# A gated delta rule inside a two-block network: readers of solved blocks queued behind the weights, the last solve level applied to the values, decay rows broadcast by DMA

## The chip, the cores and the metric

The kernel runs on one core of a Trainium2 chip. The metric is the device time of one execution in microseconds; the program has no second core to wait for. The engines are named as in the profile: PE is TensorE, DVE is VectorE, ACT is ScalarE, POOL is GpSimd, SP is the engine whose queue issues most DMAs. PEld is the weight load of PE.

## The reference, cut to what matters

Two transformer-like blocks over 256 tokens of width 2048. The change touches only the gated delta rule of the first block: 8 heads of dimension 128, chunks of 64 in the reference (the kernel takes chunks of 128, two per head).

```python
def chunk_gated_delta_rule(q, k, v, g, beta):
    ...
    gc = jnp.cumsum(g, axis=-1)
    gamma = jnp.exp(jnp.where(causal, gc[..., :, None] - gc[..., None, :], -jnp.inf))
    kb = k * beta[..., None]
    a_mat = jnp.where(strict, jnp.einsum('bhncd,bhnsd->bhncs', kb, k) * gamma, 0.0)
    t_mat = lax.linalg.triangular_solve(eye + a_mat, eye, left_side=True, lower=True, unit_diagonal=True)
    u = jnp.einsum('bhncs,bhnsv->bhncv', t_mat, v * beta[..., None])
    w = jnp.einsum('bhncs,bhnsk->bhnck', t_mat, kb * jnp.exp(gc)[..., None])
    qk = jnp.einsum('bhncd,bhnsd->bhncs', q, k) * gamma
    ...
    def step(state, xs):
        v_new = u_n - jnp.einsum('bhck,bhkv->bhcv', w_n, state)
        o = jnp.einsum('bhck,bhkv->bhcv', qg_n, state) + jnp.einsum('bhcs,bhsv->bhcv', qk_n, v_new)
        state = state * gl_n[..., None, None] + jnp.einsum('bhck,bhcv->bhkv', kd_n, v_new)
```

q, k and v come from a matmul, a causal convolution of width 4 and SiLU; q and k are l2-normalised per token. The result is rms-normed, multiplied by SiLU(z) and projected. Around it stand an attention branch, a feed-forward block, and a second block with sparse attention and retention, all untouched.

## The kernel before

All large weights stream from DRAM in granules of 128 x 1024 fp32. `load_w` takes each granule through three steps: an SP DMA into `w` (4 buffers), an ACT copy to the rounded half `wh` (3 buffers), a DVE subtraction to the rest `wl` (4 buffers). One output chunk of 128 x 256 is two granules and 48 matmuls (`wh` with both halves of the activations, `wl` with one).

**The order on PE is written out by hand.** Everything that is not a weight matmul (the delta rule, attention) is a generator; `tick` runs one step of one due generator after each group of three weight matmuls. A generator says with `yield x` when it is due next, in planner microseconds. The planner's clock advances with each matmul by columns / 2400 us, times 4 for plain fp32. So a chunk is 5.12 planner microseconds. `finish(t)` runs generators, jumping the clock to their due times with no weight matmul between, until `t` is done. The other engines' queues are ordered by a scheduler that has its own estimate of each duration and puts an instruction where it believes it to be ready; each engine then works its queue strictly in order. `behind()` adds an edge: an instruction of the block comes after the last traced granule's instruction on the same engine.

**The delta rule.** For each head `gdn_scores` squares k and q (ACT), sums the squares over the head dimension by four one-column matmuls (`tok_sums`, into `cs`), makes the decay rows `pr` by two matmuls with the gate column broadcast as weights, adds the mask, exponentiates them into `gam`, and multiplies k·k and k·q (`k0`, `k1`) by them into `S`. Four heads form a group. `gdn_solve` moves the 32 x 32 diagonal blocks of the group's S through DRAM into `X` on 32 partitions (POOL DMAs), eliminates them in 30 steps of two POOL instructions (L805, L806), and moves them back into S (L808, L810). Its planner distances are 8 for the way in, 1.3 a step, 8 for the way back. Then `gdn` runs per head: `level(0)` masks the solved blocks out of S (DVE, L829), DE = I - them (L834), PE transposes of DE, two merging levels (32 to 64 to 128), then the values: W0 = E0 V0, Y = V1 - S1 W0, W1 = E1 Y, the output `po`, its norm (with one POOL power, `f`), and transposes back. Heads 0 and 1 of a group run in lockstep, and heads 2 and 3 after them; each step is PE work and then an ACT or DVE instruction that reads its PSUM bank.

`mixers` runs group 0's scores, its values (and `a_block(1)`), group 1's scores, its values, `a_block(2)`, then the attention heads. `finish` of heads 0 and 1 of group 0 stands in front of the third head of group 1, because of S's three buffers.

Of the kernel before, what the change touches and what calls it, by code (L numbers as in the profile page):

```python
# [23 lines left out]
EPS = 1e-6  # L24
# [101 lines left out]
class Net:  # L126
# [386 lines left out]
    def mixers(self, bo, b1):  # L513
        nc, tmp, a = self.nc, self.tmp, self.a
# [74 lines left out]
        groups = []  # L589
        for p in range(2):  # L590
            hh = range(4 * p, 4 * p + 4)
            group = Group(hh)
            S = []
            for i, h in enumerate(hh):
                kq = b1.tile([P, 2, T], F32, tag="kq", name="kq", bufs=2)
                for j, dst in ((1, kq[:, 0]), (0, kq[:, 1])):
                    part(dst, j, h)
                if i >= 2:
                    self.finish(group.scores[i - 2])
                if i % 2 == 0:  # L600
                    if p and i:
                        for t in groups[0].heads[:2]:
                            self.finish(t)
                    S.append(b1.tile([P, 2, 6, P], F32, tag="gS", name="gS", bufs=3))
                group.scores.append(self.add(self.gdn_scores(h, kq, S[i // 2][:, i % 2], group)))
            group.solve = self.add(self.gdn_solve(S, group))
            for i, h in enumerate(hh):
                v = b1.tile([P, T], F32, tag="v", name="v", bufs=1)
                if p and i >= 1:
                    self.finish(groups[0].heads[i - 1])  # L610
                z = b1.tile([P, T], F32, tag="z", name="z", bufs=5)
                part(v, 2, h)
# [84 lines left out]
    def gdn_gates(self, ps, r):  # L697

        nc, b1 = self.nc, self.b1
        self.beta = b1.tile([P, H, 2], F32, name="beta")  # L700
        g = b1.tile([P, 2, H], F32, name="g")
        x = b1.tile([P, 2, H], F32, name="dl")
        e = b1.tile([P, 2, H], F32, name="de")
        for tt in range(2):
            nc.vector.tensor_scalar(self.beta[:, :, tt], ps[tt][:, 0:8], r[:, tt:tt + 1], None, op0=OP.mult)
            nc.vector.scalar_tensor_tensor(x[:, tt], ps[tt][:, 8:16], r[:, tt:tt + 1], self.row[:, 8:16],
                                           op0=OP.mult, op1=OP.add)
# [10 lines left out]
        self.g = g  # L718
        self.gcol = b1.tile([P, 3, H], F32, name="gcol")
        yield 10.0  # L720
        pc = self.aux([P, 3, H])
        lmid = self.c1("lcm")[:, P:2 * P]
        self.mm(pc[:, 0], lmid, g[:, 0])
# [8 lines left out]
    def gdn_scores(self, h, kq, S, pair):  # L732

        nc = self.nc
        sq = self.gtile(0, "sq", [P, 2, T])
        nc.scalar.activation(sq, kq, ACT.Square)
        yield 4.0 if h else 5.0

        pc = self.tok_sums([sq[:, 0], sq[:, 1]])
        cs = self.gtile(h, "cs", [P, 4])  # L740
        nc.vector.tensor_scalar(cs, pc, EPS, None, op0=OP.add)
        cp = self.b1.tile([P, 4], F32, tag="gcp", name="gcp", bufs=8)
        pair.cp[h] = cp
        self.pow(cp, cs, "mix")
        acol = self.gtile(h, "ac", [P, 2])
        nc.vector.reciprocal(acol, cs[:, 0:2])
        nc.vector.tensor_tensor(acol, acol, self.beta[:, h], op=OP.mult)

        pr = self.aux([P, 3, P])
        lcm = self.c1("lcm")  # L750
        g0 = self.g[:, 0, h:h + 1].to_broadcast([P, P])
        g1 = self.g[:, 1, h:h + 1].to_broadcast([P, P])
        self.mm(pr[:, 0], g0, lcm[:, P:2 * P])
        self.mm(pr[:, 1:3].rearrange("p a b -> p (a b)"), g1, lcm)
        gam = self.gtile(h, "gam", [P, 3, P])
        nc.vector.tensor_tensor(gam[:, 0::2], pr[:, 0::2], self.c1("gmask").unsqueeze(1).to_broadcast([P, 2, P]), op=OP.add)
        for i, j in ((0, 0), (1, 2), (2, 1)):
            nc.scalar.activation(gam[:, i], pr[:, 1] if i == 1 else gam[:, i], ACT.Exp, bias=self.gcol[:, j, h:h + 1])
        yield 2.5
        k0 = self.aux([P, 2, 2, P])  # L760
        kqf = kq.rearrange("p a t -> p (a t)")
        self.mm(k0.rearrange("p a b c -> p (a b c)"), kq[:, 0, 0:P], kqf)
        nc.vector.scalar_tensor_tensor(S.rearrange("p (x y) c -> p x y c", y=2)[:, 0::2], k0, acol[:, 0:1],
                                       gam[:, 0:2].unsqueeze(1).to_broadcast([P, 2, 2, P]), op0=OP.mult, op1=OP.mult)
        yield 0
        k1 = self.aux([P, 2, P])
        for i in range(2):
            self.mm(k1[:, 1 - i], kq[:, 0, P:T], kq[:, i, P:T])
        nc.vector.scalar_tensor_tensor(S[:, 2:4], k1, acol[:, 1:2],
                                       gam[:, 2:3].to_broadcast([P, 2, P]), op0=OP.mult, op1=OP.mult)  # L770

# [13 lines left out]
    def gdn_solve(self, S, group):  # L785


        nc, b1 = self.nc, self.b1
# [13 lines left out]
        for j in range(1, 31):  # L802
            t = tmp[:, 0:j * (31 - j)].rearrange("p (s c) -> p s c", s=j)
# [4 lines left out]
        nc.gpsimd.dma_start(Df, X)  # L808
        for d, y in diag:
            nc.gpsimd.dma_start(y, d)  # L810
        yield 8.0
        group.solved = True

    def gdn(self, h, S, group, before):
        nc, b1 = self.nc, self.b1
        z = group.z[h]
        tl = lambda tag, shape: self.gtile(h, tag, shape)
# [3 lines left out]
        cp, V = group.cp[h], group.V[h]  # L821

        B = S[:, 0::3]
        idb = self.c0("ident").unsqueeze(1).to_broadcast([P, 2, P])

        def level(l):
            m = self.lev[:, l * P:(l + 1) * P].unsqueeze(1).to_broadcast([P, 2, P])
            bm = tl("bm", [P, 2, P])
            nc.vector.tensor_tensor(bm, B, m, op=OP.mult)  # L829
            return bm  # L830

        bm = level(0)
        DE = tl("DE", [P, 2, 2, P])
        nc.vector.tensor_tensor(DE[:, 1], idb, bm, op=OP.subtract)  # L834
        yield 3.5
        pd = self.aux([P, 2, P])
        for tt in range(2):
            self.tr(pd[:, tt], DE[:, 1, tt])
        nc.scalar.copy(DE[:, 0], pd)
        for l in (1, 2):  # L840
            bm = level(l)
            yield 2.8
            pr = self.aux([P, 2, P])
            for tt in range(2):
                self.mm(pr[:, tt], bm[:, tt], DE[:, 0, tt])
            R = tl("R", [P, 2, P])
            nc.scalar.copy(R, pr)
            yield 2.4
            pu = self.aux([P, 2, 2, P])
            last = l == 2  # L850
            for tt in range(2):
                if not last:
                    self.mm(pu[:, 0, tt], DE[:, 1, tt], R[:, tt])
                self.mm(pu[:, 1, tt], R[:, tt], DE[:, 1, tt])
            if last:
                nc.vector.tensor_tensor(DE[:, 1], DE[:, 1], pu[:, 1], op=OP.subtract)
            else:
                nc.vector.tensor_tensor(DE, DE, pu, op=OP.subtract)
        E = DE[:, 1]
        W = tl("bm", [P, 2, P])  # L860
        yield 2.8
        pw = self.aux([P, P])
        self.mm(pw, E[:, 0], V[:, 0])
        nc.scalar.copy(W[:, 0], pw)
        yield 1.9
        px = self.aux([P, P])
        self.mm(px, S[:, 1], W[:, 0])
        Y = tl("Y", [P, P])
        nc.vector.tensor_tensor(Y, V[:, 1], px, op=OP.subtract)
        yield 1.9  # L870
        pw = self.aux([P, P])
        self.mm(pw, E[:, 1], Y)
        nc.scalar.copy(W[:, 1], pw)
        yield 1.9
        po = self.aux([P, 2, P])
        self.mm(po[:, 0], S[:, 4], W[:, 0])
        self.mm(po[:, 1], S[:, 5], W[:, 0], start=True, stop=False)
        self.mm(po[:, 1], S[:, 2], W[:, 1], start=False, stop=True)

        so = tl("so", [P, 2])  # L880
        dump = tl("Y", [P, P])
        for tt in range(2):
            nc.scalar.activation(dump, po[:, tt], ACT.Square, accum_out=so[:, tt:tt + 1])
        f = tl("f", [P, 2])
# [2 lines left out]
        nc.vector.tensor_scalar(so, so, SC * SC / P, EPS, op0=OP.mult, op1=OP.add)  # L887
        self.pow(f, so, "rsqrt")
        nc.vector.scalar_tensor_tensor(f, f, SC, cp[:, 2:4], op0=OP.mult, op1=OP.mult)
        on = tl("R", [P, 2, P])  # L890
        for tt in range(2):
            nc.scalar.mul(on[:, tt], po[:, tt], f[:, tt:tt + 1])
        yield 5.2
# [1 line left out]
        for tt in range(2):  # L895
            self.tr(pt[:, tt], on[:, tt])
        nc.vector.scalar_tensor_tensor(z, pt.rearrange("p a b -> p (a b)"), self.col("gnorm", 0), z,
                                       op0=OP.mult, op1=OP.mult)
# [573 lines left out]
```

## Time and profile before

| | us |
|---|---|
| median of 3 runs | 2533.32 (2533.11 to 2533.87) |
| the profiled execution | 2533.55 |
| its span | 2531.7 |
| PE busy | 2454.0 (97%) |
| DVE busy | 1905.9 (75%) |
| ACT busy | 1391.4 (55%) |
| POOL busy | 140.6 (6%) |

The span runs from the first to the last instruction of the profiled execution; its own time holds 1.85 us more around it. Busy time of PE is the time in which at least one matmul was under way. The delta rule lies in the first 500 us of the span.

### The profile page before, as it was taken

The numbers are of one execution on the slowest core, as the hardware profiler recorded it, in microseconds if no ns is written. First come the engines' busy times: TensorE is split into PE (matmuls) and PEld (weight loads), VectorE is DVE, ScalarE is ACT, GpSimd is POOL, SyncE is SP. The second block draws the span as 40 slices with busy tenths as digits, with TensorE's granted clock in tenths as the row PEclk, the third lists the DMA queues.
The fourth block names the chain that finished last, engine by engine and source line by source line (L and its number), as shares of the span: only waits on it lengthen the run. The fifth ranks groups of instructions, "written<-read, shape, count | busy, mean of one in ns | idle before, by whom it ended". The sixth has DMA issues, their size and how long they took to land.

```text
span 2531.7 us, 50856 instructions
## 1 busy us (share of the span) xinstructions
PE 2454.0 (97%) x20026; PEld 2438.4 (96%) x20026; DVE 1905.9 (75%) x3673; ACT 1391.4 (55%) x2208; POOL 140.6 (6%) x215
## 2 busy tenths in 40 slices
PE   8959779999999999999999999999999999999999
PEld 8959779999999999999999999999999999999999
DVE  7747567667788988888877678898888677666664
ACT  7626446544444556777754456654844556475443
POOL 0341610000000000000000000000000000000000
PEclk9979989999999999999999999999999999999999
DMA  6545474588898766766767767768677555455555
GB/s 219 192 148 168 137 229 143 183 266 300 295 299 297 225 223 209 239 221 210 243 215 211 242 216 218 216 211 266 211 245 236 179 183 174 152 169 171 176 184 159
DMA packets 190224, 536.66 MB, mean 212 GB/s; under 512 B 22176, under 2 KB 27680, under 8 KB 189984
## 3 DMA queue, kind: packets, MB, share of 16 engines
q1 hardware_dynamic: 188768, 532.36, 65.5%
q8 instruction: 157, 2.57, 0.4%
q0 software_dynamic: 1216, 1.05, 0.2%
q14 instruction: 83, 0.68, 0.1%
HBM read 530.70 MB, written 2.62 MB: 211 GB/s over the span
## 4 chain that ended last, share of the span: by engine, by line
PE 89%; DVE 3%; POOL 3%; DMA 2%; issue 1%; ACT 1%; SPq 0%; DVEq 0%; ACTq 0%; POOLq 0%
PE mm L186 84%; PE aux L186 4%; POOL gX L806 2%; POOL gXt L805 1%; DVE wl L223 1%; PE aux L190 1%; ACT wh L222 1%; DVE mw L1094 0%; DVE isc L1304 0%; DMA gX<-gD 0%; DMA w<-wA 0%; DMA gD<-gS 0%; DMA mc<-c 0%; DMA gD<-gX 0%; DMA mw<-wM 0%
## 5 line engine op out<-in xcount | busy, mean ns | idle before, releaser
L222 ACT CAST wh<-w 128x1024 fp32r<-128x1024 f32 (+5 forms) x867 | 854.0, 986 | 938.0 <-PE mm L186 771.4
L186 PE MATMUL mm<-u,wh 128*128 128x256 f32 (+1 forms) x7488 | 1361.9, 284 | 0.0
L223 DVE TENSOR_TENSOR wl<-w,wh 128x1024 fp32r<-128x1024 f32 (+5 forms) x867 | 993.6, 1147 | 400.6 <-ACT wh L222 396.1
L186 PEld LDWEIGHTS mm<-u,wh 128*128 128x128 f32 x7488 | 1152.8, 189 | 3.3 <-issue 2.4
L186 PE MATMUL mm<-u,wl 128*128 128x256 f32 (+1 forms) x3744 | 1053.9, 281 | 51.7 <-DVE wl L223 51.7
L186 PEld LDWEIGHTS mm<-u,wl 128*128 128x128 f32 x3744 | 706.9, 189 | 52.1 <-DVE wl L223 52.1
L186 PE MATMUL mm<-v,wh 128*128 128x256 f32 (+1 forms) x4096 | 743.4, 283 | 0.0
L186 PEld LDWEIGHTS mm<-v,wh 128*128 128x128 f32 x4096 | 629.3, 189 | 1.4 <-issue 1.0
L186 PE MATMUL mm<-v,wl 128*128 128x256 f32 (+1 forms) x2048 | 576.2, 281 | 1.6 <-DVE wl L223 1.4
L186 PEld LDWEIGHTS mm<-v,wl 128*128 128x128 f32 x2048 | 385.8, 188 | 2.6 <-DVE wl L223 2.6
L1094 DVE CUSTOM_DVE_ANT_0 mw<-mw,mc,mod 128x512 f32<-128x512 f32 x192 | 145.0, 759 | 2.9 <-ACT mc L1076 2.1
L1094 DVE CUSTOM_DVE_ANT_0 mw<-mw,mc,part 128x512 f32<-128x512 f32 x192 | 142.2, 747 | 2.7 <-ACT mc L1076 2.7
L186 PE MATMUL mm<-wh,u 128*128 128x412 f32 (+1 forms) x320 | 83.4, 339 | 0.0
L1052 ACT ACTIVATE leaf<-bit,row,dr 128x384 f32<-128x384 f32 x120 | 78.9, 699 | 0.0
L186 PE MATMUL mm<-wh,v 128*128 128x412 f32 (+1 forms) x256 | 71.8, 359 | 5.7 <-ACT wh L222 5.7
L694 DVE SCALAR_TENSOR_TENSOR u<-mm,par,u 128x255 f32<-128x255 f32 (+1 forms) x160 | 76.4, 477 | 0.7
L335 POOL TENSOR_TENSOR rc<-rc,cst 128x2 f32<-128x2 f32 x4 | 3.7, 928 | 1296.2 <-DVE rc L388 1296.2
L186 PE MATMUL mm<-more,wh 128*128 128x256 f32 x384 | 69.8, 281 | 0.0
L186 PEld LDWEIGHTS mm<-more,wh 128*128 128x128 f32 x384 | 59.1, 189 | 0.0
L186 PEld LDWEIGHTS mm<-wh,u 128*128 128x128 f32 x320 | 58.3, 188 | 0.2
L186 PEld LDWEIGHTS mm<-wh,v 128*128 128x128 f32 x256 | 50.2, 200 | 6.8 <-ACT wh L222 6.6
L1056 DVE COPY_PREDICATED leaf<-bit,leaf 128x384 f32<-128x384 uint32 x88 | 53.5, 608 | 2.5 <-ACT leaf L1052 1.9
(297 smaller groups left out, 1996.2 us busy)
## 6 DMA issues: line engine op xcount, KB each, us to landing
w<-wB SPq DMA_DIRECT2D x344, 512.0 KB, 3.9
mw<-wM SPq DMA_DIRECT2D x384, 256.0 KB, 4.0
w<-wUp SPq DMA_DIRECT2D x170, 512.0 KB, 4.0
w<-wO SPq DMA_DIRECT2D x96, 512.0 KB, 4.2
w<-wDn SPq DMA_DIRECT2D x64, 384.0 KB, 3.6
w<-wDn SPq DMA_DIRECT2D x64, 320.0 KB, 3.5
w<-wA SPq DMA_DIRECT2D x48, 412.0 KB, 3.2
w<-wBr SPq DMA_DIRECT2D x32, 512.0 KB, 4.4
```

What stands on the lines that cost most here:

```text
L186: self.nc.tensor.matmul(out, l, r, start=start, stop=stop)
L190: self.nc.tensor.transpose(out, in_, self.c0("ident"))
L222: i1 = nc.scalar.copy(h[:, :n], w[:, :n])
L223: i2 = nc.vector.tensor_tensor(l[:, :n], w[:, :n], h[:, :n].bitcast(F32), op=OP.subtract)
L335: self.nc.gpsimd.tensor_tensor(out, in_, e, op=OP.pow)
L694: nc.vector.scalar_tensor_tensor(dst[:, s:], ps[:, :T - s], tap(width - 1 - s), dst[:, s:], op0=OP.mult, op1=OP.add)
L805: nc.gpsimd.tensor_tensor(t, col, row, op=OP.mult)
L806: nc.gpsimd.tensor_tensor(X[:, 0:j, j + 1:32], X[:, 0:j, j + 1:32], t, op=OP.subtract)
L1052: nc.scalar.activation(t, bits[0], ACT.Identity, scale=dr[:, i, h:h + 1], bias=rb[:, i, 0, h:h + 1])
L1056: nc.vector.copy_predicated(t, bits[l].bitcast(mybir.dt.uint32), u)
L1094: self.nc.vector.tensor_tensor_reduce(w, w, c, 1.0, src, OP.mult, OP.add, dst)
```

## The change

- `gdn_scores`: the decay rows of all heads are made once, in `gdn_gates`, by two matmuls with 8 gate columns as weights, copied to SBUF, written to DRAM (POOL DMA), and read back per head by one DMA that broadcasts a row of 384 to 128 partitions: on POOL's queue for heads 0 to 3, on SP's for heads 4 to 7. Only q is squared and summed; k's sums of squares are read off the diagonal of k·k by two DVE multiply-and-reduce instructions with the identity. The generator has one wait where it had three.
- `gdn_solve`: the last planner distance is 18.0 where it was 8.0.
- `gdn`: level 0 and DE stand inside `behind()`; the transpose of DE (whose 32 x 32 diagonal blocks alone are not zero) is one DVE instruction. Level 1 updates DE[:, 1] only. Level 2 is not merged into E; W = E Y, then W - E (B W) for each of the two chunks, Y being kept in V.
- `mixers`: the scores of head h - 2 are finished ahead of head h's matmuls, over the groups.

```diff
+                if h >= 2:
+                    self.finish((groups + [group])[(h - 2) // 4].scores[(h - 2) % 4])
...
-                if i >= 2:
-                    self.finish(group.scores[i - 2])
...
         yield 10.0
+        pr = self.aux([P, 3 * P])
+        lcm = self.c1("lcm")
+        self.mm(pr[0:H, 0:P], g[:, 0], lcm[:, P:2 * P])
+        self.mm(pr[0:H, P:3 * P], g[:, 1], lcm)
+        rows = self.pw.tile([P, 1024], F32, tag="w", name="grow", bufs=4)
+        nc.scalar.copy(rows[0:H, 0:3 * P], pr[0:H])
+        self.grow = self.dram.tile([H, 3 * P], F32, name="grow")
+        nc.gpsimd.dma_start(self.grow, rows[0:H, 0:3 * P])
...
-        sq = self.gtile(0, "sq", [P, 2, T])
-        nc.scalar.activation(sq, kq, ACT.Square)
-        yield 4.0 if h else 5.0
-        pc = self.tok_sums([sq[:, 0], sq[:, 1]])
...
-        self.mm(pr[:, 0], g0, lcm[:, P:2 * P])
-        self.mm(pr[:, 1:3].rearrange("p a b -> p (a b)"), g1, lcm)
...
+        gam = self.gtile(h, "gam", [P, 3, P])
+        sq = self.gtile(0, "sq", [P, T])
+        nc.scalar.activation(sq, kq[:, 1], ACT.Square)
+        (nc.sync if h >= 4 else nc.gpsimd).dma_start(gam.rearrange("p a b -> p (a b)"), self.grow[h:h + 1].to_broadcast([P, 3 * P]))
+        yield 4.0 if h else 6.0
+        nc.vector.tensor_tensor(gam[:, 0::2], gam[:, 0::2], self.c1("gmask")..., op=OP.add)
...
+        pc = self.tok_sums([sq])
+        dump = self.gtile(0, "dump", [P, P])
+        for tt, kk in ((0, k0[:, 0, 0]), (1, k1[:, 1])):
+            nc.vector.tensor_tensor_reduce(dump, kk, self.c0("ident"), 1.0, EPS, OP.mult, OP.add, cs[:, tt:tt + 1])
+        nc.vector.tensor_scalar(cs[:, 2:4], pc, EPS, None, op0=OP.add)
...
-        yield 8.0
+        yield 18.0
         group.solved = True
...
-        bm = level(0)
         DE = tl("DE", [P, 2, 2, P])
-        nc.vector.tensor_tensor(DE[:, 1], idb, bm, op=OP.subtract)
-        yield 3.5
-        pd = self.aux([P, 2, P])
-        for tt in range(2):
-            self.tr(pd[:, tt], DE[:, 1, tt])
-        nc.scalar.copy(DE[:, 0], pd)
-        for l in (1, 2):
+        with self.behind():
+            bm = level(0)
+            nc.vector.tensor_tensor(DE[:, 1], idb, bm, op=OP.subtract)
+            nc.vector.transpose(DE[:, 0]..., DE[:, 1]...)
+        for l in (1,):
             bm = level(l)
-            yield 2.8
+            yield 4.0
...
+        for tt in range(2):
+            pw = self.aux([P, P])
+            self.mm(pw, E[:, tt], Y[:, tt])
+            nc.scalar.copy(W[:, tt], pw)
+            yield 1.9
+            pw = self.aux([P, P])
+            self.mm(pw, bm[:, tt], W[:, tt])
+            nc.scalar.copy(Z[:, tt], pw)
+            yield 1.9
+            pw = self.aux([P, P])
+            self.mm(pw, E[:, tt], Z[:, tt])
+            nc.vector.tensor_tensor(W[:, tt], W[:, tt], pw, op=OP.subtract)
+            yield 1.9
+            if tt == 0:
+                px = self.aux([P, P])
+                self.mm(px, S[:, 1], W[:, 0])
+                nc.vector.tensor_tensor(V[:, 1], V[:, 1], px, op=OP.subtract)
+                yield 1.9
```

## Rows read from the trace of the kernel before

**Rows 1.** Page: the span, and busy time of PE.
```profile
span 2531.7 us, 50856 instructions
PE 2454.0 (97%) x20026; PEld 2438.4 (96%) x20026; DVE 1905.9 (75%) x3673; ACT 1391.4 (55%) x2208; POOL 140.6 (6%) x215
```

**Rows 2.** Windows: length; PE, PEld, DVE, ACT, POOL busy; PE clock; DMA share; GB/s.
```profile
140.00:160.00 20.00, 0.00 (x0) 0.00 (x0) 1.57 (x5) 0.00 (x0) 15.04 (x32) 0.50 0.06 13
...
500.00:520.00 20.00, 20.00 (x171) 20.00 (x170) 8.36 (x8) 8.19 (x10) 0.00 (x0) 1.00 0.66 203
```

**Rows 3.** Timeline of PE, the two long stops: start, length, instruction, [idle before <-releaser].
```profile
161.06 0.58 PE L186 MATMUL mm<-u,wl 128*128 128x256 f32 x1 [26.39 <-DVE wl L223]
...
163.78 0.41 PE L186 MATMUL mm<-u,wl 128*128 128x256 f32 x1
...
328.51 0.58 PE L186 MATMUL mm<-u,wl 128*128 128x256 f32 x1 [25.26 <-DVE wl L223]
```

**Rows 4.** Timeline of DVE around the two stops.
```profile
126.67 1.53 DVE L223 TENSOR_TENSOR wl<-w,wh 128x1024 fp32r<-128x1024 f32 x1 [0.64 <-ACT wh L222]
...
158.43 0.76 DVE L829 TENSOR_TENSOR gbm<-gS,lev 128x256 f32<-128x256 f32 x2 [29.16 <-DMA gS<-gD]
...
325.89 0.43 DVE L829 TENSOR_TENSOR gbm<-gS,lev 128x256 f32<-128x256 f32 x1 [27.96 <-DMA gS<-gD]
```

**Rows 5.** Timeline of POOL, the solve of group 0.
```profile
109.81 0.87 POOL L805 TENSOR_TENSOR gXt<-gX 32x30 f32<-32x30 f32 x1 [3.92 <-DMA gX<-gD]
...
115.22 1.36 POOL L806 TENSOR_TENSOR gX<-gX,gXt 32x130 f32<-32x130 f32 x1
...
130.49 0.60 POOL L805 TENSOR_TENSOR gXt<-gX 32x234 f32<-32x234 f32 x1
...
138.92 0.59 POOL L805 TENSOR_TENSOR gXt<-gX 32x228 f32<-32x228 f32 x1
...
148.27 0.44 POOL L806 TENSOR_TENSOR gX<-gX,gXt 32x130 f32<-32x130 f32 x1
...
151.56 0.25 POOL L806 TENSOR_TENSOR gX<-gX,gXt 32x30 f32<-32x30 f32 x1
```

**Rows 6.** Timeline of PE: the transposes of DE, groups 0 and 1.
```profile
202.89 0.38 PE L190 MATMUL aux<-cst,gDE 128*128 128x128 f32 x2
...
203.35 0.29 PE L186 MATMUL mm<-u,wl 128*128 128x256 f32 x1
...
370.38 0.38 PE L190 MATMUL aux<-cst,gDE 128*128 128x128 f32 x2
```

**Rows 7.** Timeline of PE: sums and decay rows of one head, a pair of merging matmuls.
```profile
92.89 1.05 PE L186 MATMUL aux<-cst,gsq 128*128 128x1 f32 x8
93.81 0.90 PE L186 MATMUL aux<-cst,g 128*128 128x128 f32 x4
94.36 0.59 PE L186 MATMUL mm<-u,wh 128*128 128x256 f32 x2
...
247.12 0.39 PE L186 MATMUL aux<-gDE,gR 128*128 128x128 f32 x2
247.34 0.39 PE L186 MATMUL aux<-gR,gDE 128*128 128x128 f32 x2
```

**Rows 8.** Timeline of PE: three of the waits inside the delta rule's steps.
```profile
223.97 0.49 PE L186 MATMUL aux<-gbm,gS 128*128 128x128 f32 x2 [0.68 <-ACT gbm L864]
...
275.05 0.59 PE L190 MATMUL aux<-cst,gR 128*128 128x128 f32 x2 [2.06 <-ACT gR L892]
...
420.55 0.49 PE L186 MATMUL aux<-gY,gDE 128*128 128x128 f32 x2 [1.41 <-DVE gY L869]
```

**Rows 9.** Timeline of POOL: the power `f` of head 3.
```profile
273.69 0.70 POOL L335 TENSOR_TENSOR gf<-gso,cst 128x2 f32<-128x2 f32 x1 [0.56 <-DVE gso L887]
```

**Rows 10.** DMA issues: transfer, queue, count, KB each, median us to landing.
```profile
gX<-gD POOLq DMA_DIRECT2D x2, 128.0 KB, 4.3
posi<-positions SPq DMA_DIRECT2D x2, 128.0 KB, 4.9
```

More of the change, by code (lines that the diff above doesn't have):

```diff
@@ L734, in gdn_scores @@
         nc = self.nc
-        sq = self.gtile(0, "sq", [P, 2, T])
-        nc.scalar.activation(sq, kq, ACT.Square)
-        yield 4.0 if h else 5.0
-        pc = self.tok_sums([sq[:, 0], sq[:, 1]])
-        cs = self.gtile(h, "cs", [P, 4])
-        nc.vector.tensor_scalar(cs, pc, EPS, None, op0=OP.add)
+        gam = self.gtile(h, "gam", [P, 3, P])
[3 more added lines that the diff above has]
+        yield 4.0 if h else 6.0
+        nc.vector.tensor_tensor(gam[:, 0::2], gam[:, 0::2], self.c1("gmask").unsqueeze(1).to_broadcast([P, 2, P]), op=OP.add)
+        for i, j in ((0, 0), (1, 2), (2, 1)):
+            nc.scalar.activation(gam[:, i], gam[:, i], ACT.Exp, bias=self.gcol[:, j, h:h + 1])
+        cs = self.gtile(h, "cs", [P, 4])
+        k0 = self.aux([P, 2, 2, P])
+        self.mm(k0.rearrange("p a b c -> p (a b c)"), kq[:, 0, 0:P], kq.rearrange("p a t -> p (a t)"))
+        k1 = self.aux([P, 2, P])
+        for i in range(2):
+            self.mm(k1[:, 1 - i], kq[:, 0, P:T], kq[:, i, P:T])
+        pc = self.tok_sums([sq])
[3 more added lines that the diff above has]
+        nc.vector.tensor_scalar(cs[:, 2:4], pc, EPS, None, op0=OP.add)
+        acol = self.gtile(h, "ac", [P, 2])
+        nc.vector.reciprocal(acol, cs[:, 0:2])
+        nc.vector.tensor_tensor(acol, acol, self.beta[:, h], op=OP.mult)
         cp = self.b1.tile([P, 4], F32, tag="gcp", name="gcp", bufs=8)
@@ L744, in gdn_scores @@
         self.pow(cp, cs, "mix")
[L745 to L752, printed above, removed]
-        self.mm(pr[:, 0], g0, lcm[:, P:2 * P])
-        self.mm(pr[:, 1:3].rearrange("p a b -> p (a b)"), g1, lcm)
[L755 to L762, printed above, removed]
         nc.vector.scalar_tensor_tensor(S.rearrange("p (x y) c -> p x y c", y=2)[:, 0::2], k0, acol[:, 0:1],
                                        gam[:, 0:2].unsqueeze(1).to_broadcast([P, 2, 2, P]), op0=OP.mult, op1=OP.mult)
[L765 to L768, printed above, removed]
         nc.vector.scalar_tensor_tensor(S[:, 2:4], k1, acol[:, 1:2],
@@ L830, in level @@
             return bm
-        bm = level(0)
         DE = tl("DE", [P, 2, 2, P])
-        nc.vector.tensor_tensor(DE[:, 1], idb, bm, op=OP.subtract)
-        yield 3.5
-        pd = self.aux([P, 2, P])
-        for tt in range(2):
-            self.tr(pd[:, tt], DE[:, 1, tt])
-        nc.scalar.copy(DE[:, 0], pd)
-        for l in (1, 2):
+        with self.behind():
+            bm = level(0)
+            nc.vector.tensor_tensor(DE[:, 1], idb, bm, op=OP.subtract)
+            nc.vector.transpose(DE[:, 0].rearrange("p a b -> p (a b)"), DE[:, 1].rearrange("p a b -> p (a b)"))
+        for l in (1,):
             bm = level(l)
-            yield 2.8
+            yield 4.0
             pr = self.aux([P, 2, P])
@@ L848, in gdn @@
             yield 2.4
-            pu = self.aux([P, 2, 2, P])
-            last = l == 2
+            pu = self.aux([P, 2, P])
             for tt in range(2):
[L852 to L858, printed above, removed]
+                self.mm(pu[:, tt], R[:, tt], DE[:, 1, tt])
+            nc.vector.tensor_tensor(DE[:, 1], DE[:, 1], pu, op=OP.subtract)
         E = DE[:, 1]
-        W = tl("bm", [P, 2, P])
+        bm = level(2)
+        W = tl("W", [P, 2, P])
+        Z = tl("R", [P, 2, P])
+        Y = V
         yield 2.8
[L862 to L874, printed above, removed]
+        for tt in range(2):
[16 more added lines that the diff above has]
+                yield 1.9
         po = self.aux([P, 2, P])
@@ L880, in gdn @@
         so = tl("so", [P, 2])
-        dump = tl("Y", [P, P])
+        dump = DE[:, 0, 0]
         for tt in range(2):
@@ L889, in gdn @@
         nc.vector.scalar_tensor_tensor(f, f, SC, cp[:, 2:4], op0=OP.mult, op1=OP.mult)
-        on = tl("R", [P, 2, P])
+        on = Z
         for tt in range(2):
```

## The prediction

> **What bounds the kernel now.** I read the page first. PE is busy 2454.0 of 2531.7 us [rows 1], so only two things can pay: less work for PE, or the 77.7 us in which it has none. Next the busy time in windows of 20 us, to find where these lie. In the feed-forward part PE is full: 171 matmuls in 20 us, 0.117 us each. Between 140 and 160 us it does nothing, at a granted clock of 0.5 (1.2 of 2.4 GHz), while POOL is busy 15 of the 20 us [rows 2]. Then the timeline of PE: it stops twice, 26.39 and 25.26 us, each time for `wl`, a weight rest that DVE makes [rows 3]. So 51.65 of the 77.7 us are two stops with one form. After the first one the clock comes back late: from 161.06 to 163.78 us there are 12 matmuls in 2.72 us, 1.3 us more than 12 times 0.117 [rows 2, 3]; I take the same for the second.
>
> Why is `wl` late? The timeline of DVE: it ends a `wl` at 128.2 us and then sits for 29.16 us in front of L829, the masking of solved blocks, until the DMA that returns them has landed; 27.96 us in group 1 [rows 4]. DVE works in order, so the next `wl`, whose data have long been there, stands behind L829. POOL works at the elimination all that time, to 151.81 us [rows 5]. From its place in the queue, the scheduler must have thought the solve done by 129 us; the chip needs to 158. PE itself doesn't want the blocks yet: the transposes of DE come at 202.9 us [rows 6], 41.8 us after it starts again. The stop is therefore a matter of queue order, not of data.
>
> **The change part by part.**
>
> *The readers behind the weights, and 18.0 for 8.0.* The edge puts L829 behind the `wl` of the granule that PE is using when the planner reaches the step. Without the stop, the transposes of group 0 would stand at 202.9 - 26.4 - 1.3 = 175.2 us of PE's time. Level 0 is 3.5 planner us ahead of them. A planner microsecond is 48 x 0.117 / 5.12 = 1.10 us, so that is 171.3. Ten planner us more make 182.3. DVE runs ahead of PE: the last `wl` ended at 128.2 us, and PE stopped at 161.06 - 26.39 = 134.67, after the 24 matmuls (2.8 us) of that granule, so `wl` was ready 3.7 us ahead of its first use [rows 3, 4]. PE may be anywhere in the granule, so DVE comes to L829 at 182.3 - 3.7 = 178.6 us at the latest and 2.8 earlier, 175.8, at the earliest.
>
> When are the blocks back? Not at 158.4 us, because the stop that I take away had freed POOL. With DVE busy, one step of 130 elements took 1.36 us; with DVE stopped, the same size took 0.44. Steps 1 to 12 took from 109.81 to 130.49, 20.7 us, nearly all beside a working DVE; steps 19 to 30, of the same sizes in reverse, took from 138.92 to 151.81, 12.9 us, with DVE still [rows 5]. The ratio is 1.6. The 18 steps from 130.49 to 151.81 (21.3 us) become 34, so the solve ends 12.8 us later, at 171.2 us.
>
> The Trainium skill's page "SBUF — State Buffer", section "Who interferes with whom", gives the reason: a VectorE instruction with two SBUF inputs and a GpSimd instruction that reads SBUF shut each other out for their whole length. The trace agrees (1.36 against 0.44 us), and by that rule the gain carries part of its own undoing.
>
> Against 171.2 us DVE has 5 to 7 us in hand, and PE some 3 more before it runs dry. With the old 8.0, DVE would come 11 us sooner, at 164.8 to 167.6, 4 to 6 us too early. So the 10 are needed and suffice by a little. Group 1 by the same steps: back at 325.89 + 12.8 = 338.7; transposes at 370.4 - 26.6 = 343.8, level 0 at 343.8 + 1.1 x (10 - 3.5) = 351.0, DVE there at 344.5 to 347.3, 6 to 9 us in hand [rows 4, 6]. I take both stops as gone: 26.39 + 25.26 + 2.6 = **-54.3**. Bounds: 0, if the reader still comes too early, and -54.3.
>
> *Less work for PE.* In the scores of a head, eight records of one-column matmuls take 92.89 to 93.81, 0.92 us, and half go: 0.46. The decay rows take 93.81 to 94.36, 0.55, and go [rows 7]. That is 1.01 x 8 = 8.1 us. The shared rows are two matmuls of the same widths, once: +0.55. In `gdn`, two transposes go: 202.89 to 203.35 is 0.46 us with two ordinary matmuls (0.234) in it, so 0.23 [rows 6]. Six merging matmuls of 128 columns go (two of level 1, four of level 2) and four come; one takes 247.12 to 247.34, 0.22 us [rows 7]. So 0.23 + 2 x 0.22 = 0.67 a head, 5.4 in all. Sum **-12.9**. Lower bound of this gain: what falls into stretches in which PE waits anyway counts for nothing, which I price at none or half (6.5).
>
> *The chain gets later and longer.* Ten planner us more stand ahead of group 0's heads, but `finish` of heads 0 and 1 stays where it was, after the first two chunks of group 1's third head. What isn't done by then runs with no weights beside it. Before, the output and norm were left, with a wait such as 0.68 us [rows 8]. Now the remaining steps are those of 10 planner us more at 1.9 each: five trips from PE to ACT or DVE and back. Per trip I take 1 us, between the waits of 0.68 and 1.41 [rows 8]: **+5** (0 if hidden; 5 x 2.06 = 10 at the longest wait). Elsewhere the chains run beside weights. Per pair of heads there are 9 trips where there were 8, and 7 of them instead of 3 spaced by the short 1.9. Three pairs, four more tight trips each, 12 trips: most hidden under weight matmuls, some not; 0 to 12 x 0.68 = 8, and I take **+2**.
>
> *POOL's queue.* The power `f` of a head goes through POOL. Head 3's ran at 273.69 us, just ahead of the elimination of group 1, which began after its input had landed, and PE waited 2.06 us for what followed [rows 8, 9]. With one wait in the scores instead of three the solve starts some 3 us earlier against heads 2 and 3, so `f` may stand behind the first few steps; at up to 1.36 us each [rows 5], less the 5.2 planner us left for it: **+2**, 0 to 10.
>
> *The broadcast rows.* A row of 384 to 128 partitions is 192 KB. Nearest rows: 4.3 us to landing for POOL's 128 KB and 4.9 for the broadcast of positions [rows 10]. Given are 4.0 planner us, 4.4 us, and 6.0 for head 0, whose row must first be written out. DVE's addition of the mask may wait 1 to 5 us, and PE loses what exceeds its 3 in hand: **+2** for the eight heads, 0 to 8 x 2 = 16. On SP the broadcast issues between weight granules; its tile is long free by then.
>
> At nothing I cost DVE's additions (two reductions, two subtractions and a transpose a head; a two-input instruction of 128 x 256 takes 0.38 us [rows 4]; nothing shows the transpose, and I take 0.4 between 0.2 and 1.5, that of a `wl`): the cover is the 3 us that `wl` is ahead, and without it each head would cost PE about 1 us. The earlier `finish` of the scores waits for generators long done.
>
> **Sum.** 2533.55 (the profiled execution, span plus 1.85, and 0.2 above the median) - 54.3 - 12.9 + 5 + 2 + 2 + 2 = **2477** us, 2.2% faster.
>
> **The rivals.**
> - *The stop comes back in part, because the solve is slower beside a working DVE.* For: the 1.6 is measured on 12 of 30 steps, and the DMAs home have weights beside them now. Against: 5 to 9 us in hand, and 3 more until PE is dry. If the solve ends 15 us later than I reckon, each group loses 5 to 8 us, and with a late broadcast 2490 to 2512. Chance 0.12.
> - *The edge doesn't hold.* The scheduler puts L829 early all the same, or another reader (level 1's masking, outside the block) takes its place. DVE stops, POOL is fast again, and the stops stay at 26 us. Only PE's work goes: 2533.55 - 12.9 + 2 = 2523, 2520 to 2530. Against: level 1's mask shares its buffer with level 0. Chance 0.07.
> - *Slower: the power behind the solve.* If the scheduler, which has the solve some 30 us too short, puts `f` of heads 2 and 3 behind all of group 1's steps, PE waits at their transposes until the solve is done, about 12.9 + 21.3 us of steps times 1.6 = 55 us, and gives back the whole stop: 2477 + 65 with the DMAs, some 2540. It turns slower once more than about 56 us lie ahead of `f`, so nearly the whole solve. For: one queue, in order. Against: `f` becomes ready near the start of the solve. Chance 0.05.
> - *The forecast*: both stops gone, small waits: 2462 to 2490. Chance 0.76.
>
> The range of 8 in 10 takes in the forecast and the first rival: 2462 to 2512. Differences below 0.2% (5 us) can't be told from none. Faster (below 2528): 0.76 + 0.12 and most of the second rival, less a reserve for what I don't see: 0.91. Same 0.04, slower 0.05.
>
> **What would show it.** Right: no window without PE work between 130 and 340 us; L829 with an idle time of a few us at most and the `wl` of a later granule ahead of it; POOL's steps of 200 elements and more at about 1 us on average up to the end of the solve; four records of sums a head; no L806 in the chain that ended last. PE's waits inside the delta rule some 10 us in all, the most of it in front of the third head of group 1. Wrong: a wait of DVE for `gam`'s DMA above 3 us, PE waiting for ACT's `gR` behind POOL, or DVE still in front of L829.

## The result and the profile after

The changed kernel takes 2497.76 us (median of 4; 2497.02 to 2498.26), the kernel before 2533.22 on the same chip: ratio 0.986 [0.9843, 0.9877]. It is faster by 35.5 us. The forecast was 56, and its range of 2462 to 2512 us held the time, but only by the part that stood for the first rival (2490 to 2512): 2462 to 2490, for both stops gone and small waits, was missed by 8 us.

The page, the span and the engines' busy time:

```profile
span 2495.2 us, 50712 instructions
PE 2452.6 (98%) x19918; PEld 2433.2 (98%) x19918; DVE 1927.0 (77%) x3721; ACT 1389.3 (56%) x2209; POOL 174.0 (7%) x220
```

The span is 36.5 us shorter. PE has 42.6 us without work, where it had 77.7 [rows 1]. But its busy time has hardly fallen, 2454.0 to 2452.6, although 108 of its matmul records are gone. Busy time that stays while work goes means that something runs slower.

The windows show both sides. First the stretch that stood empty before, then four stretches around shorter stops:

```profile
140.00:160.00 20.00, 19.32 (x127) 18.08 (x126) 19.50 (x30) 8.27 (x17) 18.43 (x21) 1.00 0.66 200
42.00:52.00 10.00, 6.40 (x34) 6.11 (x35) 8.19 (x16) 8.13 (x15) 1.31 (x3) 0.66 0.55 179
188.00:200.00 12.00, 9.19 (x50) 7.95 (x51) 9.45 (x31) 2.54 (x5) 3.57 (x3) 0.72 0.62 193
333.00:343.00 10.00, 6.07 (x30) 5.33 (x30) 7.67 (x30) 3.85 (x15) 0.00 (x0) 0.66 0.65 209
412.00:420.00 8.00, 7.09 (x34) 6.94 (x35) 2.72 (x12) 1.25 (x5) 0.00 (x0) 0.57 0.32 98
```

From 140 to 160 us PE now works 19.32 of 20 us at full clock, where it had nothing [rows 2]. In the other four the mean granted clock is 0.57 to 0.72: part of each ran at 0.5, the 1.2 GHz level. What PE waits for there, in the view of waits up to 520 us (total, times, longest):

```profile
PE aux L186 <- ACT kq L583: 9.1, 4, 3.7
PE mm L186 <- ACT wh L222: 8.7, 4, 4.6
PE aux L186 <- DVE qkb L466: 7.7, 2, 4.7
PE aux L190 <- ACT gR L895: 4.2, 3, 2.3
PE mm L186 <- DVE wl L223: 3.1, 4, 1.6
```

No wait is above 4.7 us. The first is for a head's SiLU (`kq`), the third for the rotation of an attention head (`qkb`), the fourth for a head's normed output (`gR`) ahead of its transposes. The second holds the kernel's start (4.62 us, 4.67 in the kernel before), but also a stop for weights at 44 us. Its timeline, with what SP's queue waited for just ahead of it:

```profile
44.00 0.79 PE L186 MATMUL mm<-v,wh 128*128 128x256 f32 x2 [3.10 <-ACT wh L222]
46.40 0.58 PE L186 MATMUL mm<-v,wl 128*128 128x256 f32 x1 [1.60 <-DVE wl L223]
```

```profile
SPq L219 <- DMA grow<-grow: 9.1, 1, 9.1
```

SP's queue held a weight transfer for 9.1 us until the shared rows had been written out: their staging tile is one of the four buffers of the weights' ring. ScalarE, from 80 to 87 us, shows a second cause:

```profile
80.39 1.28 ACT L751 ACT_TABLE_LOAD   x1
81.68 0.40 ACT L751 ACTIVATE ggam<-ggam,gcol 128x128 f32<-128x128 f32 x1
81.99 1.03 ACT L222 CAST wh<-w 128x1024 fp32r<-128x1024 f32 x1
83.04 1.28 ACT L583 ACT_TABLE_LOAD   x1
84.33 0.42 ACT L583 ACTIVATE kq<-kq 128x256 f32<-128x256 f32 x1
84.77 1.28 ACT L751 ACT_TABLE_LOAD   x1
```

The decay exponentials (L751) no longer depend on PE, so they are issued between the two SiLUs of a head (L583), and each turn from one function to the other loads a table, 1.28 us. At 84.80 us PE has waited 3.74 us for the SiLU in the middle. The Trainium skill's page "ScalarE: Activation LUTs", section "Table sets: the hidden batching unit", says to do all activations of one set together; by that rule this order is the bad one, and the trace agrees, with three loads in 5.7 us. What differs from the kernel before is their place and not their number: for exponentials of the decay and SiLUs both kernels load 18 tables.

Last the place that the forecast was about: the solve of group 0 on POOL (its first step, its last instruction, its way home), and VectorE's reader in both groups.

```profile
114.25 0.23 POOL L808 TENSOR_TENSOR gXt<-gX 32x30 f32<-32x30 f32 x1 [2.45 <-DMA gX<-gD]
...
168.42 1.29 POOL L809 TENSOR_TENSOR gX<-gX,gXt 32x30 f32<-32x30 f32 x1
170.01 0.54 POOL L811 DMA_DIRECT2D gD<-gX  x1 [0.31 <-POOL gX L809]
175.65 3.92 POOL L813 DMA_DIRECT2D gS<-gD  x7 [5.10 <-DMA gD<-gX]
180.49 0.55 POOL L813 DMA_DIRECT2D gS<-gD  x1 [0.92 <-issue]
```

```profile
182.84 0.76 DVE L832 TENSOR_TENSOR gbm<-gS,lev 128x256 f32<-128x256 f32 x2 [3.04 <-DMA gS<-gD]
...
327.02 0.76 DVE L832 TENSOR_TENSOR gbm<-gS,lev 128x256 f32<-128x256 f32 x2 [3.62 <-DMA gS<-gD]
```

The reader waits 3.04 and 3.62 us where it waited 29.16 and 27.96 [rows 4]. POOL's steps take 114.25 to 169.71, 55.5 us, where they took 42.0 beside a VectorE that stood still for the second half [rows 5].

### The profile page after: what moved, and what is told of

Same layout as the page of the kernel before. It is cut to its first block, busy times and chain, and to the rows that moved or that the text cites. A ratio compares the mean times of both kernels' runs of the same rounds, so it can differ in the third digit from the quotient of the medians.

```text
span 2495.2 us, 50712 instructions
## 1 busy us (share of the span) xinstructions
PE 2452.6 (98%) x19918; PEld 2433.2 (98%) x19918; DVE 1927.0 (77%) x3721; ACT 1389.3 (56%) x2209; POOL 174.0 (7%) x220
## 4 chain that ended last, share of the span: by engine, by line
PE 87%; DVE 4%; POOL 3%; ACT 2%; DMA 2%; issue 1%; SPq 0%; POOLq 0%; DVEq 0%; ACTq 0%
PE mm L186 83%; PE aux L186 4%; DVE wl L223 1%; POOL gXt L808 1%; POOL gX L809 1%; ACT wh L222 1%; DVE mw L1097 1%; PE aux L190 0%; DMA ggam<-grow 0%; DVE isc L1307 0%; DMA gD<-gS 0%; DMA gX<-gD 0%; ACT L583 0%; DMA w<-wA 0%; DMA gS<-gD 0%
## 5 line engine op out<-in xcount | busy, mean ns | idle before, releaser
L1097 DVE CUSTOM_DVE_ANT_0 mw<-mw,mc,mod 128x512 f32<-128x512 f32 x192 | 151.1, 790 | 3.5 <-ACT mc L1079 2.4
```

Source lines behind the costliest of these rows:

```text
L1097: self.nc.vector.tensor_tensor_reduce(w, w, c, 1.0, src, OP.mult, OP.add, dst)
```

## The experiments

The theory for the first four: the missing 20 us went into small stops, each at a place of its own and with its own cause, and into the half clock behind them. Rival: the later and longer chain of the values took them. Each ratio is to the kernel before on the same chip, whose medians were 2533 to 2537 us.

**e1: the kernel before, with the order edit alone.**

```
-        bm = level(0)
         DE = tl("DE", [P, 2, 2, P])
-        nc.vector.tensor_tensor(DE[:, 1], idb, bm, op=OP.subtract)
+        with self.behind():
+            bm = level(0)
+            nc.vector.tensor_tensor(DE[:, 1], idb, bm, op=OP.subtract)
...
-        yield 8.0
+        yield 18.0
```

> The kernel before with nothing but the queue edge on level 0 and 18.0 for 8.0. Small-stops theory (the two long stops were worth 54 us, and what is missing in the change's gain was lost to short stops that its other parts start, each with a stretch at half clock behind it): 2533 - 54 + 5 for the later finish + 4 for the late return = 2480 to 2490, so faster than the whole change although PE has 12.9 us more to do. Chain theory (the missing gain lies in the later and slower solve and in the later heads themselves): 2505 to 2512, the change's 2498 plus the work that PE isn't spared.

2495.70 us, 0.984 [0.9825, 0.9854]. The queue order gives all of the gain; the rest of the change, with 12.9 us less work, adds nothing that can be told from none. Both ranges were missed, the small-stops theory's by 6 us and the chain theory's by 9: the order edit makes small stops too. The largest are at the rotations of the attention heads (5.03 and 3.01 us for `qkb`), where the kernel before has none.

**e2: the shared rows staged in the second `gam` tile**, outside the weights' ring.

```
-        rows = self.pw.tile([P, 1024], F32, tag="w", name="grow", bufs=4)
+        rows = self.gtile(1, "gam", [P, 3, P]).rearrange("p a b -> p (a b)")
```

> The changed kernel with the shared rows staged in the second gam tile and not in a buffer of the weights' ring. Small-stops theory: SP's wait of 9.1 us for that buffer goes, with it PE's stops of 3.10 and 1.60 us at 44 us and the half clock from 44 to about 51 us (some 3 us): 2488 to 2492. Chain theory: PE is held elsewhere in that stretch by ScalarE and VectorE, 2496 to 2498.

2489.06 us, 0.9815 [0.9801, 0.983], as the small-stops theory had it. The window in which the stop at 44 us stood:

```profile
42.00:52.00 10.00, 9.54 (x77) 8.85 (x75) 6.90 (x15) 6.74 (x14) 1.83 (x3) 1.00 0.49 145
```

PE starts 77 matmuls where it started 34, at full clock.

**e3: the exponentials behind the square of the keys.**

```
-        nc.scalar.activation(sq, kq[:, 1], ACT.Square)
+        last = nc.scalar.activation(sq, kq[:, 1], ACT.Square)
...
+        with self.tc.issue_after(last.ins):
             for i, j in ((0, 0), (1, 2), (2, 1)):
                 nc.scalar.activation(gam[:, i], gam[:, i], ACT.Exp, ...)
```

> The changed kernel with the three exponentials of a head behind the square of the same head on ScalarE, so that they no longer stand between the two SiLUs of its k and q. Small-stops theory: about half of the 18 table loads go, and PE's four waits for SiLU (9.1 us) with the half clock behind two of them (84 to 88 and 188 to 200 us, 4 us): 2484 to 2490. Chain theory: VectorE's waits for the later gam take their place, 2494 to 2500.

2489.75 us, 0.9814 [0.9798, 0.983], inside the small-stops theory's range. The stops for the SiLU near 68, 85 and 101 us are gone; one of 2.82 us at 182 stays. But the table loads are not halved: 16 of the 18 are still there, eight of each kind for eight heads. So it is their place between the SiLUs that costs.

**e4: decay rows by two matmuls of TensorE in each head**, so neither staging nor broadcast, and exponentials that wait for PE.

```
-        (nc.sync if h >= 4 else nc.gpsimd).dma_start(gam..., self.grow[h:h + 1].to_broadcast(...))
+        pr = self.aux([P, 3, P])
+        self.mm(pr[:, 0], self.g[:, 0, h:h + 1].to_broadcast([P, P]), lcm[:, P:2 * P])
+        self.mm(pr[:, 1:3]..., self.g[:, 1, h:h + 1].to_broadcast([P, P]), lcm)
```

> The changed kernel with the decay rows made by two matmuls a head as before, no DMA for them. PE has 8 x 0.55 - 0.55 = 3.9 us more to do. Small-stops theory: the weights' ring is whole again (-8) and the exponentials wait for PE again (-4 to -10): 2484 to 2492, faster than the change in spite of more work. Chain theory: 2500 to 2503.

2484.51 us, 0.9794 [0.978, 0.9809], in the small-stops theory's range: better than the broadcast it replaces, with 3.9 us more work for PE.

**e5 and e6: 24.0 and 8.0 for the solve's 18.0**, one number each in the line that ends the solve.

> The changed kernel, with 24.0 for 18.0 as the estimated length of the solve's way home. Return theory (the solved blocks come back about 6.5 us later than in the kernel before, 182.84 against about 171 to 176, so VectorE stands 3.04 and 3.62 us at the first level's product, and what queues up behind it makes TensorE's stops near 188 to 192 and 330 to 337 us, with half clock behind them): both waits of VectorE under 0.5 us, those stops shorter by 3 us or more, time 0.3 to 0.5% under the changed kernel, ratio 0.981 to 0.983. Rival (the reach is paid for in the planner: readers planned later leave less room ahead of the next stage, and stops come back there): ratio 0.986 to 0.990.

2496.63 us, 0.9848 [0.9834, 0.9863]. VectorE's wait for the blocks is gone at one of the two places and 3.0 us at the other, and nothing is gained: the stop at an attention head's scores, 4.68 us in the changed kernel, is 6.97 us here (at 335.71). Neither range holds the ratio; the theory of the late return fell, and the rival's stop at the next stage is there, but not its price.

> The changed kernel, with 8.0 for 18.0. My theory (the edge orders the readers behind what is issued before them, but only a late enough place in that order covers the solve): the readers are planned some 10 us earlier, VectorE waits some 12 to 14 us for the solved blocks at each of the two pairs of groups, and TensorE stops for some 8 to 12 us there, with half clock behind it: 2510 to 2525 us, ratio 0.991 to 0.997. Rival (the edge alone carries it, the longer estimate is not needed): ratio 0.983 to 0.987.

2501.64 us, 0.9871 [0.9855, 0.9888]. VectorE's waits and TensorE's stops, from their timelines:

```profile
182.51 0.76 DVE L832 TENSOR_TENSOR gbm<-gS,lev 128x256 f32<-128x256 f32 x2 [7.23 <-DMA gS<-gD]
...
329.11 0.43 DVE L832 TENSOR_TENSOR gbm<-gS,lev 128x256 f32<-128x256 f32 x1 [9.08 <-DMA gS<-gD]
```

```profile
187.63 0.58 PE L186 MATMUL mm<-u,wl 128*128 128x256 f32 x1 [6.47 <-DVE wl L223]
...
332.71 0.58 PE L186 MATMUL mm<-u,wl 128*128 128x256 f32 x1 [7.06 <-DVE wl L223]
```

Ten planner us less move VectorE's arrival by only 4.5 us (182.51 - 7.23 = 175.28 against 182.84 - 3.04 = 179.80). The two stops come, the stops of the same stretches in the changed kernel go, and the intervals of the two kernels overlap. My theory's 12 us didn't come. The rival's range ends at 0.987, inside this interval, though the reader's waits did grow: the reach matters a little at most.

**e7: without the edge**, 18.0 kept.

```
-        with self.behind():
+        if True:
```

> The changed kernel without the edge behind the instructions already issued; 18.0 stays. My theory (the readers of the solved blocks need nothing else, so VectorE's list takes them ahead of the conversions of weights wherever it has nothing due): the waits of some 28 us of VectorE and the stops of some 25 us of TensorE come back in both places, 2540 to 2550 us, ratio 1.003 to 1.007. Rival (the planner's place is enough, the edge does nothing): ratio 0.983 to 0.987.

2540.73 us, 1.0023 [1.0013, 1.0032]: a little slower than the kernel before, and just under my theory's range. Both long stops are back:

```profile
166.04 0.58 PE L186 MATMUL mm<-u,wl 128*128 128x256 f32 x1 [25.00 <-DVE wl L223]
...
330.44 0.58 PE L186 MATMUL mm<-u,wl 128*128 128x256 f32 x1 [25.96 <-DVE wl L223]
```

```profile
164.09 0.76 DVE L832 TENSOR_TENSOR gbm<-gS,lev 128x256 f32<-128x256 f32 x2 [28.56 <-DMA gS<-gD]
```

So the edge carries the gain, and a longer estimate without it moves the reader by nothing that helps.

**e8: levels, values and order of the change, with the gates and scores of before**; the values' tile lies in the half of DE that level 1 has read.

```
-        W = tl("W", [P, 2, P])
+        W = DE[:, 0]
```

and the two functions `gdn_gates` and `gdn_scores` of the kernel before.

> The changed kernel with the gates and the scores of the kernel before (norms by sums over partitions, decay rows by TensorE in each head, exponentials behind them); so the edge, the longer estimate, the last level on the values and the transposes by VectorE, with the values' tile in the half of the doubled block that the first level has read. Theory (the shared rows and the early exponentials are what cost; the new levels save some 5 us of TensorE and cost little): 0.2 to 0.4% under the order edit alone (which was 0.984), ratio 0.980 to 0.982. Rival (the longer chain of the values, with seven stations where four were, eats the saving): ratio 0.984 to 0.987.

2500.63 us, 0.9865 [0.985, 0.9879]. The rival's number held and the theory's did not. Whether the longer chain of the values is why isn't shown, for this kernel has a stop that no other has, at the sums of squares, some 12 us behind a wait of VectorE for the blocks:

```profile
190.22 1.86 PE L186 MATMUL aux<-cst,gsq 128*128 128x1 f32 x8 [10.97 <-ACT gsq L736]
```

```profile
178.01 0.76 DVE L829 TENSOR_TENSOR gbm<-gS,lev 128x256 f32<-128x256 f32 x2 [5.70 <-DMA gS<-gD]
```

**e9: e2 and e3 together.**

> The changed kernel with both edits at once that took 8 to 9 us each: the shared rows staged in a tile of their own instead of a buffer of the weights' ring, and the exponentials behind the square of the keys. Theory (two causes at two places, the stop near 44 us and the stops near 68, 85 and 101 us): the gains add, 17 us under the changed kernel, ratio 0.977 to 0.979. Rival (both give back the same room, since what the stops of one place cost is taken in by the next): no more than the better of the two, ratio 0.981 to 0.983.

2486.57 us, 0.9808 [0.9791, 0.9824]. By the ratios the gains don't add: this one is that of either edit within its interval. By the spans of the profiled executions they nearly do, 7.2 and 6.4 us alone and 12.0 together. Runs of one kernel lie 3 to 8 us apart here, so neither is shown. The stop of 4.68 us at a rotation (323.90) is as large as ever.

**e10: e4, with the attention's older head finished behind the next head's first projection**, so that a projection lies between a head's rotation and its scores.

```
-            if h >= 2:
-                self.finish(mob[h - 2])
-            qk = b1.tile([P, 2, T], F32, tag="kq", name="qkb", bufs=2)
             for j in range(2):
                 ps = self.chunk(a["wB1"][ci], hs)
                 ci += 1
+                if j == 0:
+                    if h >= 2:
+                        self.finish(mob[h - 2])
+                    qk = b1.tile([P, 2, T], F32, tag="kq", name="qkb", bufs=2)
```

> The kernel whose decay rows TensorE makes in each head, with one more edit: in the attention's loop the older head is finished behind the next head's first projection instead of ahead of it, so that a projection of TensorE lies between a head's rotation and its scores. Theory (the stops of 4.68 and 3.00 us at the scores, and the half clock behind them, are lost time): both gone, 8 to 11 us less, ratio 0.975 to 0.977. Rival (the time comes back at the next stage, as it did where the solve was given more time): ratio 0.978 to 0.981.

2472.78 us, 0.9749 [0.9735, 0.9764]: 11.7 us under e4. By the code, `finish` took the planner's clock past the due time of the next head's scores, so that these were issued right behind the chunk that they need; the edit that puts a chunk between takes both stops away (one of 2.83 us comes, behind the attention's `ssm`).

**e11: norms only**, that is e4 with the levels of e1.

> The order edit with the scores of the changed kernel (keys' norms off the diagonals, one square) and decay rows by TensorE in each head, but the levels as before: all three on the blocks, transposes by TensorE, the edge around the first product. It is the fourth of a square with the order edit alone (0.984), the levels alone (0.9865) and both (0.9794). Theory (the new levels lose some 5 us, by the longer chain of the values, wherever they stand): faster than both together, ratio 0.975 to 0.978. Rival (what the levels alone lost was one stop of 10.97 us at the sums of squares, which this form of the scores does not have, and the levels are worth their 5 us of TensorE): slower than both together, ratio 0.980 to 0.983.

2487.52 us, 0.9812 [0.9793, 0.9831]. With e1 (0.984), e8 (0.9865) and e4 (0.9794) this makes a square, but for one thing: e1 keeps the old place of `finish` in `mixers`, and the other three have the new one. The new levels lose 0.25% on the old scores and win 0.18% on the new ones. The rival's number held, but the intervals of each of these pairs overlap, and so do those of e1 and e11. Only the new scores on the new levels (e8 to e4) gain by more than the intervals, and e8 is the kernel with the stop of 10.97 us. That an edit's worth depends on the stops that it makes more than on its own work fits this, and is not shown by it.

**e12: the changed kernel with the edits of e2, e3 and e10**, nothing undone.

> The changed kernel with the three edits that take small stops away, and nothing of its parts undone: the shared rows staged in a tile of their own, the exponentials behind the square of the keys, and the attention's older head finished behind the next head's first projection. Theory (what the forecast left out are these stops and the half clock behind them, and nothing else of size): about 11 us under the kernel with the first two alone (0.9808), at the forecast of 2477 us for the changed kernel, ratio 0.975 to 0.978. Rival (rows by broadcast cost more than their staging, since two matmuls per head in their place gave more than both edits together): 0.978 to 0.981.

2471.93 us, 0.9756 [0.974, 0.9772], in the theory's range. Its page, the window at the former stop, its largest waits of PE up to 520 us, and last VectorE's wait for the blocks:

```profile
span 2469.4 us, 50700 instructions
PE 2441.4 (99%) x19918; PEld 2424.6 (98%) x19918; DVE 1925.6 (78%) x3721; ACT 1385.3 (56%) x2207; POOL 175.8 (7%) x220
```

```profile
42.00:52.00 10.00, 10.00 (x81) 9.52 (x80) 7.85 (x21) 7.54 (x15) 1.31 (x3) 1.00 0.53 157
```

```profile
PE mm L186 <- ACT wh L222: 5.5, 3, 4.7
PE mm L186 <- DVE wl L223: 5.1, 6, 1.7
PE aux L186 <- ACT kq L583: 4.1, 2, 2.8
PE aux L190 <- ACT gR L897: 3.3, 1, 3.3
```

```profile
DVE gbm L834 <- DMA gS<-gD: 6.9, 2, 3.8
```

PE's busy time has now fallen by 12.6 us against [rows 1], close to the 12.9 of work that the forecast counted. VectorE still waits for the blocks as long as in the changed kernel (6.7 us there), so this wait was not what kept it from the forecast. This and e10 are the fastest of all, and their intervals overlap: with the stops gone, the broadcast costs nothing that can be told.

## Why the prediction was right, and where it was off

The mechanism was right: a queue order made the two long stops, and their end is the gain. That the range held the time is in part luck. The sum was 20 us too low; the time lies in the range of the first rival, and that rival's mechanism is not what cost (e5, e12). All kernels can be put into one account. From each trace's first 520 us I take PE's idle time (the sum of all idle times above 0.1 us in its timeline) and the cost of the half clock (in windows of 4 us: a mean granted clock c means a share 2 x (1 - c) at the lower level, and half of the busy time in that share is lost, an estimate). Both are less the values of the kernel before, 73.7 and 4.4 us. Work is the forecast's own count of what PE no longer does.

| kernel | idle | half clock | work | sum | span, measured |
|---|---|---|---|---|---|
| the change | -35.8 | +10.1 | -12.9 | -38.6 | -36.5 |
| e1, order only | -42.6 | +2.0 | 0 | -40.6 | -39.0 |
| e4, rows by PE | -47.5 | +6.3 | -9.1 | -50.3 | -49.6 |
| e6, 8.0 | -27.2 | +9.1 | -12.9 | -31.0 | -32.3 |
| e7, no edge | +10.2 | +10.7 | -12.9 | +8.0 | +6.8 |
| e10, scores later | -52.6 | +1.3 | -9.1 | -60.4 | -61.0 |
| e11, norms only | -45.0 | +3.6 | -3.7 | -45.1 | -46.4 |
| e12, three stops | -50.1 | +1.1 | -12.9 | -61.9 | -62.3 |

The sums meet the spans within 2.1 us (2.7 in the kernels not listed). Idle and busy time make up a span by definition, so what this tests is that half clock and work are the change in PE's busy time: -2.8 against -1.4 us measured in the changed kernel, -11.8 against -12.6 in e12. Each row is one execution, on chips whose medians for the kernel before differ by up to 3.7 us, so it can't close much better; nothing larger is left out.

- *The two stops*, 51.65 us of idle time: right. They are gone, by queue order (e1, e7), as said. "No window without PE work" (of 20 us), the idle time of "a few us at most" at the reader and the later `wl` ahead of it all came.
- *The solve beside a working VectorE*: right in size, 34 + 20.7 = 55 us forecast, 55.5 measured. It came home later than the 171.2 us of the forecast, at 182.84, for two reasons that it didn't count: the first step began at 114.25 instead of 109.81 [rows 5], and the way home from the last step to the reader took 13.1 us instead of 6.6. VectorE came at 179.80, and instead of "5 to 7 us in hand" it was 3 us too early. The issues of the two transfers, KB each and median us to landing, of the kernel before and then of the changed one, from 90 to 200 us:

```profile
gD<-gX POOLq DMA_DIRECT2D x1, 128.0 KB, 2.3
gS<-gD POOLq DMA_DIRECT2D x8, 16.0 KB, 1.9
```

```profile
gD<-gX POOLq DMA_DIRECT2D x1, 128.0 KB, 5.2
gS<-gD POOLq DMA_DIRECT2D x8, 16.0 KB, 5.0
```

- *"The 10 are needed and suffice by a little"*: wrong. With them the reader still waits 3 us and more in both groups; without them (e6) the ratio is 0.9871 against 0.986, each within the other's interval; with 6 more (e5) nothing is won. The reader's wait isn't what costs: in e1 and e3 its longest is 6.4 and 5.7 us, against 3.62 in the change, and e3 is faster and e1 no slower; in e12 it is 3.8 us, and the time is under the forecast.
- *Less work, -12.9*: right within 3 us. Four records of sums a head are seen where eight were, and with this count the sums above close.
- *The small waits*, +11 for chain, POOL's queue and broadcast: this term was mis-sized. As idle time they are 73.7 - 51.65 = 22.0 before and 37.9 after, +15.9. That it came near is luck, for they are at other places: the tail of heads 0 and 1, where +5 was put, has 3.2 us of waits for `gR` where it had 1.7. Instead PE waits for SiLUs behind the exponentials (9.1 us), for rotations (7.7), and for weights behind the shared rows (4.7). The rotations belong to the order edit (e1), the other two to the rest of the change.
- *The clock*: the largest miss, and no term carried it. The forecast gave back 2.6 us behind the long stops and had nothing for the half clock behind short ones. Measured it is +10.1, so 12.7 us off: with the 4.9 of the waits, 17.6 of the 19.7 us by which the span missed its forecast of -56.2; the rest is the account's own remainder.
- *The broadcast rows*: "its tile is long free" looked at the destination, and not at the tile that stages the rows, which sits in the ring that paces all weights. The forecast's sign "a wait of VectorE for `gam`'s DMA above 3 us" didn't come (2.5 us in three waits); the cost stood on SP's queue.
- *The rivals*: VectorE's wait did return in part, by the later start and the way home rather than by slower steps, and it wasn't this that cost (e5, e12). The edge held (e7 shows the price if it hadn't, 2541, not 2523: small stops and half clock took more than the remaining edits saved). The power behind the solve didn't come: PE's longest wait for `gR` is 2.3 us.

Open: whether POOL's DMAs are slow through the weights' traffic or through VectorE; no run separates them. The Trainium skill's page "SBUF — State Buffer", section "Who interferes with whom", says that a DMA held up by a VectorE instruction is one whose descriptors GpSimd makes; that would fit 5.0 against 1.9 us, where VectorE and the weights had both stood still before [rows 2]. But the Trainium skill infers in the same section that a `tensor_tensor` doesn't stall a DMA, and the largest part of VectorE's work from 171 to 180 us is three of those (`wl`), so the page doesn't decide it. Whether e2's and e3's gains add is open too.

## What to carry to other kernels

When a long stop is removed, price each small stop that remains twice, once for its idle time and once for the half clock behind it: here the second was two thirds as large as the growth of the first. An operation that loses its dependence on a busy engine is issued earlier, and one queue further that can be the wrong time (table loads between two SiLUs); a staging tile from a ring that paces the weights is a wait for the weights. Where a solver's result is read in order on a shared engine, an edge in the queue decides (e7); 6 planner us more or 10 less in the estimate moved the time by no more than the intervals (e5, e6).

## What the runs showed of the hardware

A stop of 3.10 us, a short burst and another of 1.60 us are followed by half clock. It holds until about 50.5 us, 6.5 us after the restart at 44.00 (an estimate: 48 + 2 x 0.31 x 4, from the 0.69 of the third line). The windows of the changed kernel (length; PE, PEld, DVE, ACT, POOL busy; PE clock; DMA share; GB/s):

```profile
40.00:44.00 4.00, 0.90 (x8) 0.70 (x7) 3.48 (x12) 3.25 (x8) 1.06 (x2) 0.96 0.02 3
44.00:48.00 4.00, 2.40 (x9) 2.10 (x10) 2.68 (x6) 2.26 (x5) 0.77 (x2) 0.50 0.83 253
48.00:52.00 4.00, 4.00 (x27) 4.00 (x26) 3.52 (x6) 3.92 (x7) 0.00 (x0) 0.69 0.53 192
...
100.00:104.00 4.00, 2.52 (x14) 1.85 (x15) 2.06 (x8) 2.96 (x5) 0.00 (x0) 1.00 0.84 303
104.00:108.00 4.00, 4.00 (x36) 4.00 (x35) 3.00 (x7) 2.17 (x3) 3.19 (x5) 1.00 0.32 78
```

Behind the stop of 1.27 us that ended at 101.03 the clock stayed at 1.00. The transpose by VectorE, which the trace of before could not show, takes 0.43 us for 128 x 256 elements, next to the forecast's 0.4. And what VectorE's work costs POOL is seen by single instructions, here VectorE's and then POOL's of the changed kernel:

```profile
118.32 1.50 DVE L694 SCALAR_TENSOR_TENSOR v<-mm,par,v 128x255 f32<-128x255 f32 x3
160.77 1.49 DVE L223 TENSOR_TENSOR wl<-w,wh 128x1024 fp32r<-128x1024 f32 x1
```

```profile
119.18 0.40 POOL L808 TENSOR_TENSOR gXt<-gX 32x130 f32<-32x130 f32 x1
161.26 1.35 POOL L808 TENSOR_TENSOR gXt<-gX 32x130 f32<-32x130 f32 x1
```

The same product takes 0.40 us beside a step of the convolution, which reads the PSUM bank `mm`, and 1.35 us beside a `wl`, whose two inputs lie in SBUF.
